# A first k unit of 512 moving tokens in the front, and one hand-ordered section up to the first head

## Chip, core and metric

The kernel runs on one core of a Trainium2 chip. The core's engines are TensorE (PE: matmuls and PE transposes; PEld is its weight load), VectorE (DVE), ScalarE (ACT), GpSimd (POOL) and SyncE (SP, which here issues most DMAs). The metric is the time on the device in microseconds (us), taken over several runs. A profile is one execution of its own with the hardware profiler on; its span runs from the first to the last instruction of the core.

## What is computed

One layer of a hybrid block over 1024 latent tokens with a prefix of 256 context tokens (so 1280 tokens, ten tiles of 128). The input is normalised, modulated by a scale and a shift that come out of a small matrix product with the condition vector, and projected; the projection feeds a gated DeltaNet (branch A) and a differential attention (branch B):

```python
shift, scale, gate = jnp.split(jax.nn.silu(c) @ w_ada + b_ada, 3, axis=-1)
h = rms_norm(x) * (1.0 + scale[:, None]) + shift[:, None]
hc = rms_norm(ctx) * (1.0 + scale_c) + shift_c
qkv_a, z_a, a_raw, b_raw, q_b, k_b, v_b, z_b, gates = split_cols(h @ w_in)
...
qkv = jax.nn.silu(centred_conv(qkv, conv_w)).astype(jnp.float32)
```

Branch A's q, k and v pass a conv over five tokens, SiLU and (q, k) an L2 norm, before its chunked scan over eight heads in two directions. Branch B's v is only stored. All projections are taken in a split form: each operand is the sum of a high and a low part, and three matmuls (high x high, high x low, low x high) stand for one.

## The kernel before, in words

**Front** (`front`). The condition vectors, `w_ada` in four pairs of k tiles (u = 0 to 3, 256 columns each of shift and scale) and the tokens are loaded by SP. Modulation (`modulation`): for u0 and u1 a matmul with two stationary columns and 256 moving ones (`mp<-wa,cT`), for u2 and u3 a form with 32 padded columns that lie in four column groups of PE (`mp<-wa,pad`), folded by a second product. The row sums of squares are ACT's, the reciprocal root is twelve small DVE instructions per group of token tiles (`rms`, L383 to L389). The token tiles are turned by PE transposes, eight k tiles for each of three groups of tokens (0 to 3, 4 to 7, the two of context), group by group (`turns`); ACT and DVE apply the modulation as they evict (`hs`, L409; `hf`, L412), and the low part is a subtraction on DVE for even k and on POOL for odd k (L415). The matmuls of the front (`main`) are **v unit 0**: 256 columns of branch B's v and the 32 columns of the decay and beta inputs, with tokens stationary and 288 weight columns moving, ten token tiles of 24 matmuls. The first group's tiles run through k in parts of four, two and two.

**Conv section** (`conv_start`, `conv_flow`). Twelve units of 256 columns: k, q and v of branch A. Here the weights are stationary and tokens move (512, 512 and, for k and v, 256 columns), 24 matmuls for each of two column tiles and each group of tokens. Five PSUM banks (`pm`) take the results. Each column tile is copied by ACT into one of four rings (L571), goes through a tap on ACT (L581), four on DVE (L583), SiLU (L592), transposes (L597) and, for q and k, a norm, and is stored to DRAM. The ring slot of tile n waits for the stores of tile n - 4. Smaller streams run beside it: the decay (`gates`), lambda, the rotary tables and the row of output gates (`gate_row`: eight loads of 512 KB, each multiplied on DVE).

**Between the sections.** After the conv section the pools on the right are closed; the first head's preparation (`gdn_first`) is written out up to its first need of a PSUM bank (loads of X, kq; 20 Abs and two Exp on ACT), then **v unit 1** follows in plain program order (`unit`, `tok_unit` L501, `v_out` L700 to L703): ten token tiles in five banks, with one staging slot for high and one for low parts. Then the section of scans begins; its PSUM pools take the same banks, and its first product is `gram<-kq`.

**What sets the order.** Inside a `manual_schedule` block the instructions of each engine stand in the order in which a planner calls them: each piece of work is a stream of steps with an engine, a cost in us and the steps that it depends on. `turn_flow` and `flow` pick at each point the stream that can begin first, within a tolerance and by a bias. Before the section of scans the planner's clocks are set to zero. DMA issues are steps of SP's or ACT's own stream, and wait there in order. Only the order is planned: on the chip each instruction waits for semaphores.

Of the kernel before, what the change touches and what calls it, by code (L numbers as in the profile page):

```python
# [17 lines left out]
P = 128  # L18
# [25 lines left out]
class Block:  # L44
# [143 lines left out]
    def setup(self):  # L188
# [7 lines left out]
        self.fold = cp.tile([P, P], F32, name="fold")  # L196
        nc.vector.tensor_reduce(self.fold[:, :32], self.ident.rearrange("p (a i) -> p i a", i=32), AX.X, ALU.add)
        for m in range(1, 4):
            nc.vector.tensor_copy(self.fold[:, 32 * m:32 * m + 32], self.fold[:, :32])
# [37 lines left out]
    def front(self, st, early, kv0):  # L237

        nc, a, cp, V = self.nc, self.a, self.cp, self.nc.vector
        fs, ft = self.spool(st, "fs", 1, side="right"), self.spool(st, "ft", 1, side="right")  # L240
# [3 lines left out]
        for g in range(3):  # L244
            for t in groups[g]:
                xt[t] = fx[g].tile([P, D], F32, tag="x", name="x")
        rows, rw2, rw3 = (fs.tile([n, P], F32, name=i) for i, n in (("rows", 16), ("rw2", 26), ("rw3", 120)))
        smallT = cp.tile([P, 184], F32, name="smallT")
        self.gdn_g, self.diff_g = smallT[:, 40:41], smallT[:, 41:42]
        self.convw = lambda j, t: smallT[:, 64 + j * 24 + t:64 + j * 24 + t + 1]  # L250
        cT = self.cT = cp.tile([P, 16], F32, name="cT")
        c2 = cT.rearrange("p (s k) -> p s k", s=2)
        pad = fs.tile([P, KT, 32], F32, name="pad")
        mods = fs.tile([P, 2, KT, 2], F32, name="mods")
        junk = fs.tile([P, D], mybir.dt.bfloat16, name="junk")
        self.pfree, self.slot_t = [(i, None) for i in range(3)], [None, None]
        turnq, evq, wv = ([], []), [], [self.wv.tile([P, KT, W + 32], F32R, tag=t, name=t) for t in ("wh", "wl")]
        free, self.dq = [None] * self.CB, 2.0
        self.raw_t, self.parts_done, self.parts_, self.part_t = [None, None], 0, {}, {}

# [3 lines left out]
        def loads():  # L264
# [3 lines left out]
            for o in "0s1xw23yk":  # L268
# [5 lines left out]
                elif o in "0123":  # L274
                    u = int(o)
                    for i in range(2):
                        if u == 0:
                            wa[u, i] = self.wab[0].tile([P, KT, W], F32, tag=("wh", "wl")[i], name="wa")
                        elif u == 1:
                            wa[u, i] = self.hc.tile([P, KT, W], F32, tag=f"s2{i}", name="wa")  # L280
                        else:
                            if i == 0:
                                wa[u, 2] = self.hp.tile([P, KT, 512], F32, tag=f"s1{u - 2}", name="wa")
                            wa[u, i] = wa[u, 2][:, :, i * W:(i + 1) * W]
                        T["wa", u, i] = self.later((yield get(3.0, wa[u, i], a["w_ada"][0, :, i * D + u * W:i * D + (u + 1) * W].rearrange(
                            "(k p) n -> p k n", p=P))), -1.2)
                elif o == "w":
                    for s in range(2):
                        k = slice(s * KT // 2, (s + 1) * KT // 2)
                        raws[s] = raw = self.wr.tile([P, KT // 2, W + 32], F32, tag="wr", name="wr")  # L290
                        yield get(1.5, raw[:, :, :W], self.wcols(C_VB).rearrange("(k p) n -> p k n", p=P)[:, k])
                        T["wr", s] = self.later((yield get(0.3, raw[:, :, W:], a["w_in"][0, :, C_AB:C_AB + 32].rearrange(
                            "(k p) n -> p k n", p=P)[:, k])), -1.2)
                elif o == "k":
                    yield lambda: ("w", 1) in T and ("m", 0) in T
                    for s in range(2):
                        k = slice(s * KT // 2, (s + 1) * KT // 2)
                        raws[s] = raw = self.wr.tile([P, KT // 2, W], F32, tag="wr", name="wr")
                        T["kr", s] = yield get(1.5, raw, kv0.rearrange("(k p) n -> p k n", p=P)[:, k], [T["w", s]])
                else:  # L300
                    for t in (range(0, 4), range(4, NT))["xy".index(o)]:
# [3 lines left out]
        def split(dst, key, to, engs):  # L305
            yield lambda: (key, 1) in T
            ends = []
            for s in range(2):
# [7 lines left out]
                if to is T:  # L316
                    T["w", s] = [t1, t2]
# [1670 lines left out]
```

## Time and profile before

| | |
|---|---|
| time, median of 3 runs | 2059.33 us (2055.46 to 2067.66) |
| time of the profiled execution | 2050.87 us |
| its span | 2049.1 us, 38360 instructions |
| granted TensorE clock, mean over the span | 0.985 |
| HBM read and written | 222.66 MB and 112.32 MB |

The page gives the busy time of each engine and a row for each group of instructions: line, engine, operation, output<-input by the program's names, partitions x elements, count, busy time, mean duration in ns, and the idle time of the engine ahead of them with what ended it. Other views answer for a stretch: the busy times by stretch with the granted clock (1.00 is full speed), the instructions in order of time (start, duration), and the chain of work that ended last (start, duration, engine, tile, line). Matmuls overlap in their records, so their pace is read from the distance of their starts.

### The profile page before, as it was taken

To read this page: it belongs to the slowest core of one execution; us is meant where nothing else is said; L and a number is where in the kernel's file an instruction comes from. 1 tells how busy PE (TensorE), PEld (TensorE's weight loads), DVE (VectorE), ACT (ScalarE), POOL (GpSimd) and SP (SyncE) were. 2 spreads that over 40 slices of the span, in tenths; PEclk is the share of its full clock that TensorE was granted. 3 is DMA by queue.
4 is the path that set the end of the run, shared out by engine and by line. 5 is a ranking of instruction groups with operands and counts; after the bars stand their busy time and mean duration, and the time that the engine had idled before them with its cause. 6 is when DMAs were issued, how large, how long until landed. Compare 5 with 4: busy or idle time off the path is not lost.

```text
span 2049.1 us, 38360 instructions
## 1 busy us (share of the span) xinstructions
PE 1968.3 (96%) x14231; PEld 1726.7 (84%) x14231; DVE 1419.5 (69%) x3616; ACT 1053.8 (51%) x2176; POOL 682.3 (33%) x600
## 2 busy tenths in 40 slices
PE   7899999989999998999999999999999999988999
PEld 4788878889999997888787888887888888876899
DVE  4698998847876885657656786227789899874532
ACT  3354344343325443567356754547678888773210
POOL 1100000014431331323323333235566767664122
PEclk9999999999999999999999999999999999999999
DMA  9226543565446556756764764757575666325452
GB/s 316 75 91 159 152 105 87 130 179 158 137 142 207 155 180 170 231 172 213 191 223 131 258 178 146 238 146 220 155 196 134 184 190 160 99 89 194 154 155 85
DMA packets 392030, 337.50 MB, mean 165 GB/s; under 512 B 144431, under 2 KB 343697, under 8 KB 391843
## 3 DMA queue, kind: packets, MB, share of 16 engines
q1 hardware_dynamic: 328963, 275.27, 46.3%
q10 hardware_dynamic: 62880, 59.78, 9.6%
q8 instruction: 112, 1.84, 0.4%
q14 instruction: 75, 0.61, 0.1%
HBM read 222.66 MB, written 112.32 MB: 163 GB/s over the span
## 4 chain that ended last, share of the span: by engine, by line
PE 72%; DVE 10%; DMA 8%; ACT 5%; issue 2%; POOL 1%; SPq 1%; ACTq 0%; DVEq 0%; POOLq 0%
PE mm L55 40%; PE chain L55 5%; PE mo L55 4%; PE s L55 4%; PE v L55 4%; DVE S L1569 3%; PE out L55 3%; PE ma L55 3%; ACT S L1582 2%; PE t L58 2%; DMA ma<-ma 1%; PE mm L501 1%; PE gram L55 1%; DVE al L1643 1%; DMA x<-xd 1%
## 5 line engine op out<-in xcount | busy, mean ns | idle before, releaser
L55 PE MATMUL mm<-hs,wh 128*128 128x512 f32 (+1 forms) x2048 | 644.8, 389 | 0.0
L55 PEld LDWEIGHTS mm<-hs,wh 128*128 128x128 f32 x2048 | 373.2, 190 | 57.6 <-issue 0.9
L55 PE MATMUL mm<-hs,wl 128*128 128x512 f32 (+1 forms) x1024 | 400.0, 391 | 0.0
L55 PE MATMUL mm<-wh,hs 128*128 128x256 f32 (+1 forms) x1632 | 313.2, 290 | 2.6 <-DVE hs L415 2.6
L55 PEld LDWEIGHTS mm<-wh,hs 128*128 128x128 f32 x1632 | 260.8, 194 | 3.8 <-DVE hs L415 3.4
L1569 DVE TENSOR_SCALAR_CACHE_REDUCE S<-s,rsq 128x512 f32<-128x512 f32 (+1 forms) x384 | 241.7, 654 | 32.0 <-PE s L55 29.2
L55 PE MATMUL mm<-wl,hs 128*128 128x256 f32 (+1 forms) x816 | 236.1, 289 | 0.0
L1606 POOL TENSOR_TENSOR S<-S 128x1280 f32<-128x1280 f32 x64 | 188.8, 2952 | 89.3 <-ACT S L1599 81.6
L55 PEld LDWEIGHTS mm<-hs,wl 128*128 128x128 f32 x1024 | 194.6, 190 | 28.2
L1582 ACT ACTIVATE S<-S,mn 128x1280 f32<-128x1280 f32 x128 | 174.7, 1366 | 34.2 <-DVE mn L1581 33.5
L55 PEld LDWEIGHTS mm<-wl,hs 128*128 128x128 f32 x816 | 158.3, 194 | 0.3
L55 PE MATMUL s<-kk,qh 128*128 128x512 f32 (+1 forms) x384 | 145.1, 378 | 3.2 <-DVE S L1569 2.9
L583 DVE SCALAR_TENSOR_TENSOR ac<-xc,smallT,ac 128x1284 f32<-128x1284 f32 (+1 forms) x96 | 138.9, 1449 | 9.5 <-ACT ac L581 8.3
L55 PE MATMUL s<-kk,ql 128*128 128x512 f32 (+1 forms) x384 | 133.8, 359 | 0.0
L1643 DVE TENSOR_TENSOR al<-t,ah 128x512 fp32r<-128x512 f32 (+1 forms) x192 | 107.4, 593 | 9.4 <-ACT ah L1638 8.7
L571 ACT COPY xc<-mm 128x512 f32<-128x512 f32 (+1 forms) x64 | 33.9, 534 | 143.0 <-PE mm L55 133.6
L1164 DVE TENSOR_TENSOR tmp<-ab,ts 80x31 f32<-80x31 f32 (+15 forms) x248 | 100.9, 407 | 8.3 <-DMA ab<-da 2.9
L1638 ACT CAST ah<-t 128x512 fp32r<-128x512 f32 (+1 forms) x192 | 89.8, 515 | 29.0 <-PE t L58 27.8
L568 POOL MEMSET xc<- 128x2 f32 (+1 forms) x64 | 3.5, 100 | 300.6 <-ACT sq L617 152.7
L58 PE MATMUL t<-ct,S 128*128 128x128 f32 x640 | 95.8, 276 | 2.9 <-POOL S L1606 1.6
L1342 DVE SCALAR_TENSOR_TENSOR S<-S,egl,chain 128x128 f32<-128x128 f32 x128 | 43.2, 344 | 75.7 <-PE chain L55 72.7
L1329 ACT ACTIVATE vd<-chain,edk 128x128 f32<-128x128 f32 x144 | 52.2, 368 | 80.7 <-PE chain L55 77.5
(283 smaller groups left out, 4691.6 us busy)
## 6 DMA issues: line engine op xcount, KB each, us to landing
wr<-in_w_in_dram ACTq DMA_DIRECT2D x42, 512.0 KB, 5.5
hx<-in_w_in_dram ACTq DMA_DIRECT2D x64, 256.0 KB, 3.8
X<-gcd SPq DMA_DIRECT2D x16, 640.0 KB, 6.4
kd<-col SPq DMA_DIRECT2D x40, 256.0 KB, 2.5
xd<-X SPq DMA_DIRECT2D x16, 640.0 KB, 6.4
x<-xd SPq DMA_DIRECT2D x80, 128.0 KB, 2.6
kk<-kd SPq DMA_DIRECT2D x32, 320.0 KB, 7.0
wa<-in_w_ada_dram SPq DMA_DIRECT2D x8, 1024.0 KB, 7.2
```

The lines of the kernel that those rows point to most:

```text
L55: self.nc.tensor.matmul(out, lhsT, rhs, start=start, stop=stop)
L58: self.nc.tensor.transpose(out, src, self.ident[:src.shape[0], :src.shape[0]])
L571: e = yield ACT, 0.57 if m == 512 else 0.31, [t, x["old"]], lambda: nc.scalar.copy(xc[:, d:d + m], pt[:, :m])
L583: t = yield DV2, 1.21e-3 * wd, [t], lambda: nc.vector.scalar_tensor_tensor(ac[:, :wd], xc[:, j:j + wd], self.convw(j, x["ct"]), ac[:, :wd] ...
L1164: t = yield DV2, n * w / 960.0 + 0.08, [t, t1], lambda: V.tensor_tensor(tv, ab[:, j + 1:, j:j + 1].to_broadcast([80, n, w]), ts[:, j, :w]. ...
L1329: td = yield ACT, 0.251, [t], lambda: nc.scalar.activation(vd, pc[:, 1], AF.Copy, scale=self.edk[:, c, g:g + 1])
L1342: t = yield DVE, 0.263, [t], lambda: V.scalar_tensor_tensor(Sn, S, self.egl[:, c, g:g + 1], pc[:, 2], ALU.mult, ALU.add)
L1569: e = yield DVE, 0.675 if m == 512 else 0.408, [e, self.sfree[c].get(n - 4 + c)], lambda: self.nc.vector.tensor_scalar(x["S"][c][:, o:o + ...
L1582: x["x"].append((yield ACT, 1.36, [e], lambda: nc.scalar.activation(S, S, AF.Exp, bias=x["mn"][:, c:c + 1], scale=-1.0, accum_out=w["l0"][ ...
L1606: e = yield POOL, 2.9, [e], lambda: self.nc.gpsimd.tensor_tensor(S0, S0, S1, ALU.add)
L1638: e = yield ACT, 0.48 if nb == 4 else 0.27, [t, y["old", k]], lambda: self.nc.scalar.copy(y["ah", k][:, :, q], pv)
L1643: t = yield DVE, 0.603 if k < 2 else 0.322, [e, y["old", k]], lambda: self.nc.vector.tensor_tensor(y["al", k][:, :, q], pv, y["ah", k][:, ...
```

## The change

The first k unit of the conv section and v unit 0 change places. The front's matmuls are now those of the k unit, with weights stationary and a whole group of tokens moving, ordered by pairs of k tiles (`ORDER`): pair 0 for tokens 0 to 3, for tokens 4 to 7, then pair 1, and so on; the context tokens last, over all k. Transposes follow the same order. Five banks hold its results (two column tiles by two groups, and one bank for both context parts). Loads go in a new order: rows, first four x tiles, first k weights, u0, small vectors, four x tiles, u1, u2, u3, context, v's weights. All four modulation pairs take the padded form; the second half's row is evicted by ACT. The reciprocal root is taken per token tile, by POOL (an addition and a power), not on DVE.

v unit 0 becomes the second unit of the conv section (`kind == "t"`), one token tile at a time with 288 columns; its evictions are a stream of the planner, with two staging slots. v unit 1 becomes the last unit of that section, its evictions staged in the conv rings as long as these are open, or in two slots once they are closed. The first head's preparation (`first`) and the load of the rotary table are streams of the same section, which start when all conv tiles and side streams are done. The planner's clocks are not reset ahead of the scans. The gate row is made in two halves of 512 columns (sixteen loads of 256 KB). Constants that only these stages use (`fold`, `convT`, `cT`) lie in a pool of their own that is closed with them.

```diff
-            for o in "0s1xw23yk":
+            for o in "xw0sy123zv":
...
-                        t = yield PE, 0.1 if u >= 2 else 0.432, [T["wa", u, i], tc, tb], lambda: self.mm(
-                            mp[32 * j:32 * j + 32, o:o + W], pad[:, k], wa[u, i][:, k], k < 4, k >= 4) if u >= 2 else self.mm(
-                            mp[:2, o:o + W], c2[:, :, k], wa[u, i][:, k], k == 0, k == KT - 1)
-                    t = yield DVE, 0.42, [t], lambda: V.tensor_copy(mrow[:n, i], mp[:n, o:o + W])
...
+                        t = yield PE, 0.08, [T["wa", u, i], tc, tb], lambda: self.mm(
+                            mp[32 * j:32 * j + 32, o:o + W], pad[:, k], wa[u, i][:, k], k < 4, k >= 4)
...
-            for g in range(3):
...
-                    yield lambda: ("x", t) in T
-                    e = yield ACT, 1.27, [T["x", t]], lambda: nc.scalar.activation(junk, xt[t], AF.Square, accum_out=ss[:, j:j + 1])
...
+            ss, y = (fs.tile([P, NT], F32, name=i) for i in ("ss", "xry"))
+            for t in range(NT):
+                yield lambda: ("x", t) in T
+                e = yield ACT, 1.27, [T["x", t]], lambda: nc.scalar.activation(
+                    junk, xt[t], AF.Square, scale=D ** -0.5, accum_out=ss[:, t:t + 1])
+                e = yield PL1, 0.15, [e], lambda: nc.gpsimd.tensor_scalar_add(y[:, t:t + 1], ss[:, t:t + 1], EPS)
+                e = yield PL1, 0.3, [e], lambda: self.power(y[:, t:t + 1], y[:, t:t + 1])
+                T["xs", t] = yield DVE, 0.69, [e], lambda: V.tensor_scalar_mul(xt[t], xt[t], y[:, t:t + 1])
...
         def turns():
-            for g in range(3):
...
+            for g, ks in ORDER:
+                if g == 2:
+                    yield lambda: ("mm", 1) in T
+                    self.hs.get(2) or self.hgroup(2)
+                for k in ks:
+                    yield lambda: ("m", k // 2) in T and ("xs", groups[g][-1]) in T and self.pfree
...
-            n = 0
-            pts = {}
-            for ts, parts in ((range(4), (range(4), (4, 5), (6, 7))),) + tuple(((t,), (range(KT),)) for t in range(4, NT)):
...
-                            th, tl, o = self.hsel(t)
-                            for i, (ht, wt) in enumerate(((th, wv[0]), (th, wv[1]), (tl, wv[0]))):
-                                e = yield PE, 0.133, [T["h", g, k], T["w", k // 4], b], lambda: self.mm(
-                                    pt[:, :W + 32], ht[:, k, o:o + P], wt[:, k], k == i == 0, k == KT - 1 and i == 2)
...
+            pts = [self.pm.tile([P, 512], F32, tag="mm", name="mm") for _ in range(5)]
+            for g, ks in ORDER:
+                n = len(groups[g]) * P
+                for s, k in [(s, k) for s in range(2) for k in ks]:
+                    yield lambda: ("h", g, k) in T and ("w", k // 4) in T
+                    th, tl, _ = self.hsel(groups[g][0])
+                    pt = pts[4][:, s * W:s * W + W] if g == 2 else pts[2 * s + g]
+                    for i, (wt, ht) in enumerate(((0, th), (0, tl), (1, th))):
+                        e = yield PE, 0.2265 if n == 512 else 0.1195, [T["h", g, k], T["w", k // 4]], lambda: self.mm(
+                            pt, T["hl"][wt][:, k, s * P:(s + 1) * P], ht[:, k, :n], k == i == 0, k == KT - 1 and i == 2)
+                    if k == KT - 1:
+                        self.first_[s, g] = pt, e
+            self.parts_done, self.part_t[0] = 1, e
+
+        ORDER = [(g, (2 * u, 2 * u + 1)) for u in range(4) for g in range(2)] + [(2, range(KT))]
...
+        for g, b in ((self.gates(), 0.5), (self.lam_setup(), 0.6), (self.qk_tables(), 4), (self.gate_row(), 4)):
+            self.stream(self.side(g), b)
+        self.stream(self.conv_weights([c for _, c in cols], pools), 3)
         self.stream(self.conv_flow(cols), 9)
...
-        self.ahead = self.parts_.pop(last)[:2]
-        self.wab = pools if last % 2 == 0 else pools[::-1]
-        self.streams, self.now, self.dq = [], 0.0, 0.0
-        self.clk, self.port, self.table, self.heat = [0.0] * 5, [0.0, 0.0], None, 0.0
+        done = lambda: len(self.cdone) >= self.ctiles and self.sides == 4 and not self.ringed
...
+        self.stream(self.first(done, right, late), 6)
+        self.turn_flow(lambda: last in self.parts_ and self.parts_done == last and self.head and not self.evq)
...
+        self.ahead = self.parts_.pop(last)
+        self.wab = pools if last % 2 else pools[::-1]
+        self.streams = []
+
+    def side(self, g):
+        yield from g
...
+    def first(self, done, right, late):
+
+        self.head = self.late = None
+        yield done
+        for st in right:
+            st.close()
+        self.late = self.tk = late()
+        self.gdn_first()
+        g = self.preps(0)
+        x = next(g)
+        while not callable(x) or x():
+            x = next(g) if callable(x) else g.send((yield x))
+        tb = self.tk.tile([P, 2, 2, NL, 32], F32, tag="tb", name="tb")
+        self.rope["k"] = tb, (yield DMA, 1.5, [], lambda: self.nc.sync.dma_start(tb.rearrange("p a b t f -> p (a b t f)"), self.tbd[1]))
+        self.head = g, x
...
+        free, n, c = [None] * (self.CB - 5), 0, 0
...
+            if kind == "t":
+                w, nt = (W + 32, 1) if i == 1 else (W, 2)
+                for t0 in range(0, NT, nt):
...
+    def v_out(self, pair, t0, nt, pt, t, free):
+
+        nc, V, s, n = self.nc, self.nc.vector, t0 // nt % 2, W * nt
+        ring = None
+        if nt == 2:
+            yield lambda: self.late or self.ctiles + t0 // 2 - 4 in self.cdone
+            ring = None if self.late else self.ctiles + t0 // 2
+        if ring is None:
+            vt, old = [self.tk.tile([P, n], F32R, tag=f"{i}{s}", name="vt") for i in ("ch", "cl")], self.slot_t[s]
+        else:
+            self.ringed, old = self.ringed + 1, self.out_t[ring - 4]
+            vt = self.cv.tile([P, CW + 2 * PAD], F32, tag="xc", name="vx")[:, :2 * n].bitcast(F32R).rearrange("p (i c) -> p i c", i=2)
...
+        acc = cv.tile([P, 512], F32, name="gacc", bufs=1)
+        t = t1 = None
         for o in (0, 512):
...
-                self.tk = self.spool(cx, "tk2")
...
-                first, head = self.gdn_first(gr, zr)
...
-                self.unit(*v1, self.wcols(self.part_cols(*parts[0])))
...
+                cols = kv[:1] + [("t", C_VB)] + kv[1:] + [("t", C_VB + W), (None, self.part_cols(*parts[0]))]
...
+                    self.gstack = gr, zr
+                    self.conv_start(cols, (right, lc), lambda: self.spool(cx, "tk2"))
+                    first, head = self.head
```

410 lines of the change are left out of this document (175 added, 235 removed).

## The prediction

> **What bounds the kernel now.** I read the page's busy table first, then the busy times of stretches cut where the work changes, then the chain that ended last around the two places where TensorE (PE) stands idle.
>
> ```profile
> span 2049.1 us, 38360 instructions
> PE 1968.3 (96%) x14231; PEld 1726.7 (84%) x14231; DVE 1419.5 (69%) x3616; ACT 1053.8 (51%) x2176; POOL 682.3 (33%) x600
> PE 72%; DVE 10%; DMA 8%; ACT 5%; issue 2%; POOL 1%; SPq 1%; ACTq 0%; DVEq 0%; POOLq 0%
> ```
>
> PE is busy for 96% of the span and carries 72% of the last chain, so time is won only where PE idles, or runs at a low clock: 81 us are idle in all. The busy times by stretch show where (columns: stretch, length, busy time and count of PE, PEld, DVE, ACT, POOL, then granted clock, DMA share, GB/s):
>
> ```profile
> 0.00:92.89 92.89, 74.31 (x476) 55.43 (x476) 53.83 (x131) 35.50 (x59) 17.95 (x19) 0.93 0.60 200
> 92.89:410.87 317.98, 316.22 (x1590) 267.22 (x1589) 276.91 (x399) 135.43 (x161) 3.55 (x64) 1.00 0.48 121
> 410.87:439.70 28.83, 28.83 (x243) 28.83 (x242) 11.80 (x11) 10.75 (x25) 3.04 (x2) 1.00 0.74 189
> 446.91:454.90 7.99, 0.01 (x2) 0.04 (x1) 5.47 (x11) 5.94 (x14) 3.66 (x2) 0.72 0.33 110
> 454.90:460.00 5.10, 5.10 (x24) 5.10 (x25) 0.83 (x2) 0.58 (x1) 0.00 (x0) 0.50 0.48 156
> 460.00:464.00 4.00, 4.00 (x33) 4.00 (x33) 1.74 (x6) 0.92 (x3) 0.00 (x0) 0.92 0.39 131
> ```
>
> The front (v unit 0) ends at 92.89 and idles PE for 18.6 us. The twelve k, q and v units run to 410.87 with PE full, and v unit 1 to 439.70. Then comes a hole of 7.99 us, after which 5.10 us run at half clock (2.55 us lost) and 4 us at 0.92 (0.3 lost): the hole costs 10.9 us.
>
> **The change part by part.** *Unit costs.* The timeline gives PE's pace in steady work:
>
> ```profile
> 80.75 0.42 PE L55 MATMUL mm<-wh,hs 128*128 128x288 f32 x2
> 92.75 0.29 PE L55 MATMUL mm<-wh,hs 128*128 128x288 f32 x1
> 399.16 0.62 PE L55 MATMUL mm<-hs,wh 128*128 128x512 f32 x2
> 407.32 0.62 PE L55 MATMUL mm<-hs,wh 128*128 128x512 f32 x2
> 408.00 0.40 PE L55 MATMUL mm<-hs,wh 128*128 128x256 f32 x2
> 410.87 0.28 PE L501 MATMUL mm<-wh,hs 128*128 128x256 f32 x1
> ```
>
> Between the first two rows stand 90 matmuls of 288 columns in 12.00 us, so 0.133 us each; between the next two 36 of 512 columns in 8.16 us, 0.227 each; then 24 of 256 columns in 2.87 us, 0.120 each. So v unit 0 is 240 x 0.133 = 32.0 us of PE, and the first k unit 96 x 0.227 + 48 x 0.120 = 27.5 us.
>
> *The swap.* The first k unit goes into the front and v unit 0 behind it. If F is the time at which the front's last matmul ends, PE, kept full, comes to the end of v unit 1 at F + 32.0 + (317.98 - 27.5) + 28.83 = F + 351.3. Before, that was 439.70. So the swap gains 88.4 - F.
>
> *When the loads let the front end.* The DMA engines are saturated there (DMA view of the first 100 us, 40 slices of 2.5 us):
>
> ```profile
> DMA  2799999999999999999100311104003012233396
> GB/s 60 209 366 344 340 349 389 410 366 295 334 349 349 348 363 408 411 395 347 43 0 0 105 52 52 56 5 152 0 0 97 15 52 90 67 105 108 39 322 201
> ```
>
> ```profile
> wa<-in_w_ada_dram SPq DMA_DIRECT2D x8, 1024.0 KB, 7.2
> x<-in_x_dram SPq DMA_DIRECT2D x8, 512.0 KB, 10.0
> wr<-in_w_in_dram SPq DMA_DIRECT2D x4, 512.0 KB
> ```
>
> The first 17 slices sum to 14.2 MB at 42.5 us. The new order puts 13.9 MB up to the last modulation weights: constants and rows 0.3, eight x tiles 4.2, two halves of the first k weights 1.05, eight modulation loads 8.4. They land at about 42 us by the same curve. Behind them come the two context tiles and v's weights (47 to 48 us), needed later.
>
> *What PE still owes then.* In the changed kernel's order on PE, behind the last modulation product (8 matmuls, seen as 16) stand 67 of the 96 matmuls of 512 columns, 37 transposes and the 48 of 256 columns. The pieces (timeline, then the chain):
>
> ```profile
> 32.78 1.07 PE L55 MATMUL mp<-wa,pad 128*32 128x256 f32 x16 [0.79 <-DVE mods L359]
> 46.02 0.44 PE pt L58 x4
> ```
>
> That is 1.1 + 0.3 (folding) + 67 x 0.227 + 37 x 0.11 + 48 x 0.120 = 26.4 us. PE comes to that product when the weights have landed (42) and when VectorE (DVE) and GpSimd (POOL) have delivered the third k pair before it; I take 44. So F is 70.4 at full clock. By the same prices PE has only some 15 us of work between 21 and 44, so I add 2 us for a low clock: F = 72.4.
>
> *DVE beside it.* These groups of the first 93 us, by form, must fit in front of it:
>
> ```profile
> L412 DVE TENSOR_SCALAR hf<-pt,mods 128x512 f32<-128x512 f32 x16 | 12.9, 809 | 4.5 <-ACT hs L409 3.6 <-POOL hs L415 0.5
> L391 DVE TENSOR_SCALAR x<-x,xry 128x1024 f32<-128x1024 f32 x10 | 7.0, 746 | 0.0
> L415 DVE TENSOR_TENSOR hs<-hf,hs 128x512 fp32r<-128x512 f32 x8 | 5.5, 684 | 0.0
> L412 DVE TENSOR_SCALAR hf<-pt,mods 128x256 f32<-128x256 f32 x8 | 4.3, 544 | 1.0 <-ACT hs L409 0.7
> L313 DVE TENSOR_TENSOR wl<-wr,wh 128x1024 fp32r<-128x1024 f32 x2 | 2.4, 1222 | 0.0
> L353 DVE COPY mrow<-mp 128x256 f32<-128x256 f32 x4 | 1.7, 420 | 2.7 <-PE mp L55 2.7
> L415 DVE TENSOR_TENSOR hs<-hf,hs 128x256 fp32r<-128x256 f32 x4 | 1.7, 415 | 0.0
> ```
>
> From about 21.5 us (modulation of the first k pair ready) DVE owes 12.9 + 6 x 0.746 + 5.5 + 4.3 + 2.4 + 1.7 + 1.7 = 33 us, with the small modulation adds 34. Walked in its new order with its waits for landings, it is done near 62 us; 26 matmuls of 256 columns then remain (3 us). So DVE alone would allow F = 66, and PE sets F. **Bounds of F:** 66 (DVE) to 82: of PE's 26 us, 31 wide matmuls and 21 transposes (9.4 us) stand ahead of the point where the last k pair is awaited, and at half clock they would take 9.4 us more. The swap gains 88.4 - 72.4 = **16 us** (6 to 22).
>
> *The joined section.* The hole before is read from the timeline:
>
> ```profile
> 428.36 1.96 SPq L1096 DMA_DIRECT2D X<-gcd  x2
> 434.33 5.96 ACT L1113 ACTIVATE X<-X,gcc 128x128 f32<-128x128 f32 x20 [10.66 <-DMA X<-gcd]
> 444.89 0.56 ACT L700 CAST vt<-mm 128x512 fp32r<-128x512 f32 x1
> 454.10 0.69 DVE L701 TENSOR_TENSOR vt<-mm,vt 128x512 fp32r<-128x512 f32 x1 [2.29 <-DMA vd<-vt]
> 454.90 2.05 PE L55 MATMUL gram<-kq 128*128 128x128 f32 x8 [7.99 <-issue]
> ```
>
> The gram product takes the bank of v unit 1's fourth tile, and its eviction stands on ScalarE (ACT) behind the head's 20 Abs and two Exp, with one staging slot that waits for each store. In the changed order three of the five evictions stand ahead of the Abs, the fourth behind one Abs alone, and there are more slots; the gram waits for the fourth eviction and for kq. Counting from v unit 1's start, the last conv tile's stores leave at about 15 us (two evictions of 0.69 us now stand among the last taps on DVE), X is issued at 20.6, lands 6 us later as before (428.36 to 434.33), so that the fourth eviction is done at 28.4 and kq, issued 2 us behind X, lands near 31. PE arrives at 28.8. A stall of 2 to 3 us remains, against 10.9: **8 us** gained (0 to 10.9).
>
> *Edits at about nothing.* The modulation of the first two k pairs changes from 3.6 us per 16 instructions to 1.07, and the reciprocal roots move from DVE to POOL; both lie under the loads. The root on 128x1 isn't in the trace: between 0.10 us (a memset of 128x1) and 1.76 (the same operation on 128x8); I take 0.3, and even the upper end delays only the x tiles, which DVE awaits with 8 us of waits in hand. The gate row becomes 16 loads and 16 multiplies at half width, the same sum, under a DVE that has 41 us free in 318. v unit 0's evictions add 10 x (0.42 + 0.18) = 6 us of DVE to that section; where that cover is gone, PE waits for banks. From the second head on, each engine's order is that of before, so the shift should arrive at the end whole.
>
> ```profile
> 447.79 1.76 POOL L172 TENSOR_TENSOR ss<-ss,mhalf 128x8 f32<-128x8 f32 x1 [1.48 <-DVE ss L984]
> 0.72 0.10 POOL L201 MEMSET mhalf<- 128x1 f32 x1 [0.29 <-POOLq L1975]
> 19.45 3.62 PE L55 MATMUL mp<-wa,cT 128*2 128x256 f32 x16
> ```
>
> **Sum:** 16 + 8 = 24 us. The profiled execution took 2050.87 us (span 2049.1 and 1.8 around it), so 2027 on its own level. It lies 0.4% under the median of the runs shown, 2059.33 (2055.46 to 2067.66). On the median's level the forecast is **2035 us**.
>
> **The rivals.**
>
> *A, the hole stays.* kq lands late, or the head's ACT work again holds the fourth eviction. For it: X can't be issued before the last conv stores. Against: the order above. Gain 16 alone: 2043 us.
>
> *B, the front runs at half clock.* This row pair shows what it costs: three matmuls of 288 columns from 69.48 to 70.37, 0.89 us against 0.40.
>
> ```profile
> 69.48 0.85 PE L55 MATMUL mm<-wh,hs 128*128 128x288 f32 x2 [2.31 <-DVE hs L415]
> 70.37 0.68 PE L55 MATMUL mm<-wh,hs 128*128 128x288 f32 x2
> ```
>
> The new front has PE wait for pairs of loads 6 us apart until 42 us, so it may come to its 26 us of work cold and be stopped again by DVE in between. With F = 82 the gain is 6.4 + 8 = 14: 2045 us. The Trainium skill (TensorE: Matmul & The Clock Gate, section "What's actually happening") says that an idle window of about 3.4 us halves the clock and a window of sustained work restores it. By that rule, the trace agrees: the hole of 7.99 us is followed by 0.50, and full clock is back within 9 us. The same rule speaks for B where PE's gaps exceed that window, and against it from 44 us on, where PE has a queue of 26 us in front of it.
>
> *A and B together:* 6 us, 2053 us.
>
> *C, DVE chained to the v units; slower.* Fifteen evictions now stand in DVE's order among the conv taps, and each can hold DVE until its tile's matmuls end. Work of DVE from F to the end of v unit 1: 276.9 + 11.8 + 6.0 = 294.7 us, waits before 41, together 335.8 of 351.3: 15.5 us of slack. If DVE did nothing else between evictions, v unit 0 would add 32 - 6 = 26 us of waits and v unit 1 some 25: 51 us, 35.5 beyond the slack, and 11.5 more than the gain: 2071 us. It decides from 15.5 + 24 = 39.5 us of added waits. Against it: the new order on DVE puts conv taps and norms between the evictions.
>
> *The change doesn't do what it says:* 67 of the 96 wide matmuls still stand behind the last load, so "begins with" is only a third true; the forecast holds that already.
>
> **How the numbers follow.** Forecast 0.50 (own range 2026 to 2042), A 0.16, B 0.16, both 0.10, C 0.08. A measurement of this kernel can tell about 0.5%, 10 us, from no change: below 2049 is faster, above 2069.6 slower. The forecast, A and B are faster: 0.82, less 0.02 for their edges, 0.80; both together and half of C's cases within 0.5%: 0.13 with the edges; slower 0.07. The range reaches from a front at its lower bound (22) with two thirds of the hole gone, 30 us or more and some for the level, 2020, to A and B together, 2053.
>
> **What would show it.** The first 288-column matmul of v unit 0 starts at F: 72 (66 to 82), where before the first k unit started at 92.89. PE stays full from there to the gram (between F + 351 and F + 354; 454.9 before, 424 to 427 now), and the clock behind it stays near 1.00. If the time from the gram to the end differs from before's by more than 3 us, the claim that the shift arrives whole is wrong; if PE has gaps between F and the gram, C is at work.

## The result, and the profile after

| | before | changed |
|---|---|---|
| time, median | 2057.39 us (2048.15 to 2067.66, 4 runs) | 2033.60 us (2031.96 to 2036.39, 4 runs) |
| timed again later | 2056.70 us (17 runs) | 2037.30 us (2032.64 to 2040.16, 6 runs) |
| profiled execution, span | 2050.87 us, 2049.1 us | 2031.96 us, 2030.2 us |

The changed kernel is faster: the ratio is 0.9885 (95% interval 0.9835 to 0.9934), and 0.9899 (0.9878 to 0.9920) the second time, so 21 to 24 us. The forecast was 2035 us, 24 us below the 2059.33 that were known then. The ratios leave out two slow runs, 2733.54 us of the kernel before and 7830.38 us of experiment 6.

The page of the changed kernel, with its span, its busy times and the shares of the chain that ended last:

```profile
span 2030.2 us, 38407 instructions
PE 1959.4 (97%) x14239; PEld 1722.5 (85%) x14239; DVE 1407.7 (69%) x3581; ACT 1058.0 (52%) x2184; POOL 688.7 (34%) x618
PE 72%; DMA 10%; DVE 8%; ACT 5%; issue 2%; SPq 1%; POOL 1%; ACTq 0%; DVEq 0%; POOLq 0%
```

PE now idles 71 us of its span instead of 81, and its busy time is 9 us less.

Where the work changes (stretch, length, busy time and count of PE, PEld, DVE, ACT, POOL, granted clock, DMA share, GB/s), and the first rows of v unit 0, of v unit 1 and of the gram in the timeline:

```profile
0.00:74.85 74.85, 57.63 (x387) 41.61 (x388) 41.07 (x69) 36.84 (x59) 28.76 (x48) 1.00 0.67 232
74.85:395.73 320.88, 320.64 (x1687) 275.55 (x1686) 279.04 (x420) 137.43 (x169) 3.23 (x54) 1.00 0.46 118
395.73:424.50 28.77, 28.77 (x242) 28.75 (x240) 14.94 (x20) 10.93 (x20) 0.63 (x1) 1.00 0.95 236
424.50:440.00 15.50, 14.69 (x124) 14.48 (x123) 7.60 (x21) 11.51 (x30) 2.75 (x2) 1.00 0.89 300
```

```profile
74.85 0.30 PE L55 MATMUL mm<-wh,hs 128*128 128x288 f32 x1
...
395.73 0.28 PE L55 MATMUL mm<-wh,hs 128*128 128x256 f32 x1
...
420.54 0.57 ACT L546 CAST vt<-mm 128x512 fp32r<-128x512 f32 x1
...
424.55 0.46 PE L55 MATMUL gram<-kq 128*128 128x128 f32 x2
...
425.81 0.94 PE L55 MATMUL gram<-kq 128*128 128x128 f32 x6 [0.81 <-DMA kq<-gq]
```

The front's matmuls end at F = 74.85 us, v unit 1 starts F + 320.9 and ends at 424.5, where it ended at 439.70 before: the swap is worth 15.2 us there. v unit 1's fourth eviction (the CAST at 420.54) stands behind one Abs of the head, as the prediction read it from the order, and the gram follows at once, without the 7.99 us of idle and the half clock behind it; PE then waits 0.8 us for kq. Before, 7.2 us of the next unit's work stood ahead of the gram (439.70 to 446.91), so the gram's own time (30.4 us sooner) says too much. A fair mark behind the rearranged stretch is the first product of 64 columns of the first head's inverse (the first `pz<-X` on 64 rows): 619.3 us before, 595.6 now, **23.7 us**. The span is shorter by 18.9 us only, since later stages took longer; that is taken up behind experiment 8.

### The profile page after: what moved, and what is told of

The parts are those of the page before. It is cut to its first block, busy times and chain, and to the rows that moved or that the text cites. A ratio compares the mean times of both kernels' runs of the same rounds, so it can differ in the third digit from the quotient of the medians.

```text
span 2030.2 us, 38407 instructions
## 1 busy us (share of the span) xinstructions
PE 1959.4 (97%) x14239; PEld 1722.5 (85%) x14239; DVE 1407.7 (69%) x3581; ACT 1058.0 (52%) x2184; POOL 688.7 (34%) x618
## 4 chain that ended last, share of the span: by engine, by line
PE 72%; DMA 10%; DVE 8%; ACT 5%; issue 2%; SPq 1%; POOL 1%; ACTq 0%; DVEq 0%; POOLq 0%
PE mm L55 37%; PE chain L55 5%; PE mo L55 4%; PE s L55 4%; PE v L55 4%; PE m L55 4%; PE out L55 3%; PE ma L55 3%; DVE S L1557 3%; PE t L58 2%; ACT S L1570 2%; DMA wr<-in_w_in_dram 1%; DVE al L1631 1%; DMA vv<-gv 1%; PE gram L55 1%
## 5 line engine op out<-in xcount | busy, mean ns | idle before, releaser
L55 PE MATMUL mm<-wh,hs 128*128 128x256 f32 (+1 forms) x1792 | 334.8, 286 | 0.0
L55 PEld LDWEIGHTS mm<-wh,hs 128*128 128x128 f32 x1792 | 281.5, 191 | 0.4
L55 PE MATMUL mm<-wl,hs 128*128 128x256 f32 (+1 forms) x896 | 256.0, 286 | 0.0
L55 PEld LDWEIGHTS mm<-wl,hs 128*128 128x128 f32 x896 | 171.2, 191 | 0.3
L590 DVE SCALAR_TENSOR_TENSOR ac<-xc,convT,ac 128x1284 f32<-128x1284 f32 (+1 forms) x96 | 138.7, 1448 | 16.2 <-ACT ac L588 15.6
```

Source lines behind the costliest of these rows:

```text
L55: self.nc.tensor.matmul(out, lhsT, rhs, start=start, stop=stop)
L590: t = yield DV2, 1.21e-3 * wd, [t], lambda: nc.vector.scalar_tensor_tensor(ac[:, :wd], xc[:, j:j + wd], self.convw(j, x["ct"]), ac[:, :wd] ...
```

## The experiments

Twelve runs, of which 8 and 9 are the second profiles. F is read as in the prediction (the first 288-column matmul), P is the first 64-column product just named. The ratios are against the kernel before, on the same chip.

| kernel | F | gram | P | ratio of times (95%) |
|---|---|---|---|---|
| before, first and second profile | – | 454.9, 455.9 | 619.3, 619.8 | 1 |
| changed, first and second profile | 74.85, 74.23 | 424.5, 424.8 | 595.6, 595.1 | 0.9885, 0.9899 |
| 1 swap alone | 74.20 | 439.6 | 604.6 | 0.9949 (0.9933 to 0.9965) |
| 2 join alone | – | 446.9 | 617.9 | 1.0004 (0.9985 to 1.0023) |
| 3 groups, not pairs | 80.71 | 430.8 | 601.4 | 0.9916 (0.9897 to 0.9936) |
| 4 idle transposes ahead | 75.59 | 426.8 | 598.1 | 0.9909 (0.9889 to 0.9929) |
| 5 less loads | 75.56 | 426.8 | 597.2 | one run, 2041.09 us |
| 6 old modulation form | 85.63 | 434.8 | 605.4 | 0.9961 (0.9943 to 0.9979) |
| 7 idle transposes in the gaps too | 74.25 | 427.5 | 599.5 | 0.9902 (0.9873 to 0.9931) |
| 10 first modulation unit first | 76.51 | 428.0 | 600.2 | 0.9896 (0.9870 to 0.9922) |
| 11 and the second one early | 75.16 | 425.9 | 597.1 | 0.9887 (0.9862 to 0.9913) |
| 12 join alone, DVE relieved | – | 454.5 | 620.4 | one run, 2093.98 us |

**1. The swap alone.** The new front, with v unit 1 and the first head in plain program order as before:

```diff
-cols = kv[:1] + [("t", C_VB)] + kv[1:] + [("t", C_VB + W), (None, self.part_cols(*parts[0]))]
+cols = kv[:1] + [("t", C_VB)] + kv[1:] + [(None, C_VB + W)]
...
+first, head = self.gdn_first(gr, zr)
...
+self.unit(*v1, self.wcols(self.part_cols(*parts[0])))
```

> The new front with v unit 0 moved behind the first k unit, but v unit 1 and the first head's preparation outside the hand-ordered section, as before the change. Forecast's theory (two independent gains, 15 us measured for the swap and 9 us for the hole): v unit 1 still starts near 396 us, the hole before the gram comes back with 8 us of idle PE and half clock behind it, and the time is 14 to 16 us under the kernel before. Rival (the two parts need each other: the swap only fills the time in which the head's loads were waited for): under 8 us, with v unit 1 itself late. Rival (the join was worth nothing by itself): the same time as the changed kernel, 22 to 24 us under the kernel before.

Its first 64-column product comes at 604.6, 14.7 us sooner than before, and the hole is back (PE's waits between 74 and 446 us, then the stretch behind the gram's start, then the mark P):

```profile
PE gram L55 <- issue: 9.1, 1, 9.1
```

```profile
439.60:446.00 6.40, 6.35 (x31) 6.38 (x32) 1.77 (x5) 0.58 (x1) 0.00 (x0) 0.53 0.40 135
```

```profile
L55 PE MATMUL pz<-X x320: 218/218/268, 604.6 to 1273.3; 64*64 64x64 f32 x160
```

So at P the two parts of the changed kernel are 14.7 and 9.0 us, near the 16 and 8 of the forecast. In the time the swap alone shows 10.5 us (7 to 14), which misses the 14 to 16 expected; the 4 us that are lacking lie in stages behind P (1440.4 us from P to the end, against 1429.8 and 1434.8 in the two profiles of the kernel before).

**2. The join alone.** The old front, with v unit 1 and the first head in the hand-ordered section; from P on the orders of DVE, ACT and POOL are those of the changed kernel.

```diff
-self.conv_start(kv, C_VB + W)
...
+cols = kv + [("t", C_VB + W), (None, self.part_cols(*parts[0]))]
...
+self.conv_start(cols, (right, sv), lambda: self.spool(cx, "tk2"))
```

> The old front (v unit 0 first, its modulation forms and roots as before), with v unit 1 and the first head's preparation joined to the hand-ordered section. Forecast's theory: the front's PE still ends at 92.9 us, v unit 1 still ends near 440 us, and the gram follows it at once: 8 to 10 us under the kernel before, so that this and the swap alone add up to 22 to 26 us. Rival (the hole only moves, to the landing of kq or to a DVE order with more waits): 0 to 4 us.

The rival came out: nothing is gained (ratio 1.0004, P 1.4 us sooner), since DVE has an order with more waits. The profiled execution took 2065.44 us, 10 more than the median of its 12 runs; the excess lies behind P (1445.7 us from there to the end). The hole ahead of the gram is gone, but the conv section has got one of its own. PE's main waits from 90 to 450 us (`pq` is a product of the norms), the stretch that holds the first two, and rows of DVE ahead of it and in it:

```profile
PE mm L55 <- DVE wl L935: 2.7, 1, 2.7
PE pq L55 <- DVE zk L705: 2.4, 1, 2.4
PE gram L55 <- DMA kq<-gq: 0.7, 1, 0.7
```

```profile
280.00:300.00 20.00, 15.21 (x53) 12.06 (x54) 19.62 (x37) 5.28 (x7) 0.13 (x2) 0.83 0.71 157
```

```profile
257.43 0.69 DVE L692 TENSOR_SCALAR rq<-pq 32x8 f32<-32x8 f32 x4 [4.54 <-PE pq L55]
...
287.09 1.55 DVE L650 SCALAR_TENSOR_TENSOR ac<-xc,smallT,ac 128x1284 f32<-128x1284 f32 x1
...
288.79 1.22 DVE L935 TENSOR_TENSOR wl<-wr,wh 128x1024 fp32r<-128x1024 f32 x1
```

DVE is busy 19.62 of those 20 us, and the low part of the next weights (`wl`) stands behind conv taps in its queue; PE waits, and its clock falls to 0.83. P of the four kernels makes the sum: 14.7 (swap) + 1.4 (join) = 16.1, and both together 23.7. The missing 7.6 us fit this stall, 4.8 us of idle PE in these 20 us and a low clock in the rest; no run shows the join on the old front with neither the stall nor the hole. The changed kernel has 0.24 us of idle PE from F to the end of v unit 1. The forecast priced the join only on top of the swap; as a part by itself it is worth nothing here.

**12. The join alone, DVE relieved.** To see whether it is DVE's load that stalls PE there:

```diff
-                                       c0, W, [self.part_t.get(i - 2)], self.parts_, i, (DV2, DV2))
+                                       c0, W, [self.part_t.get(i - 2)], self.parts_, i, (POOL, DV2))
```

> The join alone (old front, v unit 1 and first head joined), with the low part of every unit's first half of weights subtracted on POOL, which is idle in the conv section, instead of DVE: some 13 x 1.2 us less for DVE between 93 and 440 us. The planner writes another order for the scans from this, so only the time of the first gram product is read. Theory (the old front leaves DVE behind, and PE then waits for the low parts of its weights: 5.2 us of idle PE and a low clock near 290 us): the idle goes and the gram starts at 440 to 443 us instead of 446.9. Rival (the joined order itself, not DVE's load, holds PE): 446 to 449 us.

PE's busy time of the stretch from 200 to 300 us, and from 440 to 460:

```profile
200.00:300.00 100.00, 100.00 (x496) 83.94 (x495) 89.85 (x126) 42.30 (x49) 10.60 (x20) 1.00 0.45 115
...
440.00:460.00 20.00, 14.67 (x104) 13.90 (x103) 4.00 (x13) 10.78 (x27) 0.63 (x1) 0.83 0.80 278
```

The stall in the conv section is gone (PE 100.00 of 100 us). DVE is as busy as before from 280 to 300 us (19.72 of 20 us), which speaks for the place of `wl` in its queue, behind the taps, rather than for its load as such; the edit changes the planner's order too, so this isn't fully shown. But the gram started at 454.5, not at 440 to 443, and P is 620.4, 1 us later than in the kernel before. The head's X is issued only at 444.62 us there, behind v unit 1's last store from a ring and two stores of the rotary table, and PE idles 5.3 us between 440 and 460. Half of the theory held; that the gain would then arrive didn't. The run took 2093.98 us with another order in all later stages, which says nothing on the join.

**3. Groups instead of pairs.**

```diff
-ORDER = [(g, (2 * u, 2 * u + 1)) for u in range(4) for g in range(2)] + [(2, range(KT))]
+ORDER = [(g, (2 * u, 2 * u + 1)) for g in range(2) for u in range(4)] + [(2, range(KT))]
```

> The changed kernel with the first k unit's contraction in the order of token groups (all eight k tiles of the first four token tiles, then all eight of the next four) instead of by pairs of k tiles over both groups. Theory (the pairs feed PE while the modulation weights land): work ahead of the last modulation product is only the first group's, some 28 us from 15.2 us on, so PE waits 2 to 3 us for the last weights and the front's matmuls end near 77 us instead of 74.85; 2 to 3 us slower than the changed kernel. Rival (PE has enough to do in either order): 74 to 75.5 us, no difference.

F is 80.71: the pairs are worth 6 us of F, more than the 2 to 3 expected, and not for the expected reason. In the time they are worth 3.5 us by the ratios, with intervals that overlap. From 30 us on PE waits 3 us in all, none of it for the last weights but for evictions (the longest is 1.8 us for DVE's `hf`), and it falls below full clock (0.89 between 45 and 60 us):

```profile
45.00:60.00 15.00, 12.99 (x78) 9.41 (x77) 9.25 (x14) 9.39 (x15) 7.24 (x8) 0.89 0.02 4
```

**5, 6. What sets F.** The prediction had the last modulation weights land at 42 us, and PE's remaining work behind them. Theory A is that. Theory B is that PE's own work sets F. Experiment 5 leaves out the last 2 MB of modulation weights; experiment 6 puts the first two units' products and their folding back into the old form.

```diff
+if u == 3:
+    wa[u, i] = wa[2, i]
...
```

> The changed kernel without the two loads of the fourth modulation unit's weights (2 x 1 MB): its products read the third unit's weights, so this part of the output is another. The instructions of PE, DVE, ACT and POOL stand in the same order, and the last weights land some 5 us sooner. Theory A (the last weights' landing sets the front's end): the first 288-column matmul starts at 70 to 71 us instead of 74.85. Theory B (PE's own work from 15.2 us on, a part of it at half pace, sets it): 74 to 75 us, unchanged, although the weights are there sooner.

```diff
-mp[32 * j:32 * j + 32, o:o + W], pad[:, k], wa[u, i][:, k], k < 4, k >= 4)
+mp[32 * j:32 * j + 32, o:o + W], pad[:, k], wa[u, i][:, k], k < 4, k >= 4) if u >= 2 else self.mm(
+mp[:2, o:o + W], c2[:, :, k], wa[u, i][:, k], k == 0, k == KT - 1)
```

> The changed kernel with the modulation of the first two k pairs in its form of before the change (two output rows, 3.62 us per unit half in the trace of before, against 1.94 us now), every engine's order kept. Theory A, with the prediction's step that this edit lies under the loads and is worth nothing: the front's matmuls end within 1 us of 74.85. Theory B (PE's work sets the end): four unit halves cost 1.7 us more each, the front's matmuls end at 80 to 82 us and the time is 5 to 7 us over the changed kernel's.

With less loads F stays, though DMA's traffic ends 5 us sooner (40 to 45 us: share 0.07, where the changed kernel has 1.08). The first row of v unit 0 there:

```profile
75.56 0.30 PE L55 MATMUL mm<-wh,hs 128*128 128x288 f32 x1
```

With the old form F is 85.63, 11 us later, and the kernel 12 to 13 us slower than the changed one (0.9961 against 0.9899), twice what theory B expected:

```profile
16.30 6.46 PE L55 MATMUL mp<-wa,cT 128*2 128x256 f32 x16 [10.37 <-DMA wa<-in_w_ada_dram]
23.48 3.62 PE L55 MATMUL mp<-wa,cT 128*2 128x256 f32 x16
...
34.19 4.37 PE L55 MATMUL mp<-wa,cT 128*2 128x256 f32 x16
...
85.63 0.30 PE L55 MATMUL mm<-wh,hs 128*128 128x288 f32 x1
```

The four old products take 6.46, 3.62, 4.37 and 3.62 us, where the changed kernel's take 1.94 three times and 1.07: 11.2 us more. (Each is 8 matmuls, which the trace records as 16.) Theory A falls: the landing of the last weights doesn't set F, and an edit that the prediction put at nothing is worth some 11 of the swap's 15 us. In the changed kernel PE has no idle from 30 to 60 us:

```profile
15.00:30.00 15.00, 12.74 (x71) 7.09 (x72) 7.10 (x12) 6.20 (x11) 5.98 (x9) 1.00 1.07 395
30.00:45.00 15.00, 15.00 (x133) 10.40 (x133) 8.67 (x15) 5.69 (x9) 4.66 (x4) 1.00 1.08 372
45.00:60.00 15.00, 15.00 (x95) 11.85 (x94) 11.80 (x16) 10.15 (x17) 9.10 (x8) 1.00 0.02 5
60.00:74.85 14.85, 14.61 (x93) 12.11 (x92) 7.72 (x16) 6.51 (x11) 4.15 (x15) 1.00 0.28 78
```

The fourth of these products shows where PE's work takes over. First row: the changed kernel; second: experiment 5; third: experiment 7 (below).

```profile
32.83 1.07 PE L55 MATMUL mp<-wa,pad 128*32 128x256 f32 x16
...
33.53 1.07 PE L55 MATMUL mp<-wa,pad 128*32 128x256 f32 x16
...
32.21 1.07 PE L55 MATMUL mp<-wa,pad 128*32 128x256 f32 x16
```

From its start to F it is 42.02 us in the changed kernel, 42.03 in experiment 5, 42.04 in 7, 42.00 in 4 and 41.63 in 10; in 6 it starts at 41.09 and takes 2.55 us more itself, and the distance is 44.54. So from there on PE's own work sets F, whether the loads end at 40 or at 45 us, and what moves F is the time at which PE comes to this product. (In experiment 5 it came 0.7 us later, since its first weights were there 1.3 us later.)

**4, 7, 10, 11. Can F be moved?** If PE's work from its first weights at 15.2 us sets F, then full pace from the start, or an earlier start, should bring it forward. Experiment 4 puts 60 transposes of the identity ahead of the first weights, experiment 7 puts 75 there and 47 more in the gaps until 28 us, experiments 10 and 11 load modulation weights sooner.

```diff
+for _ in range(60):
+    self.tr(wm[:, 0:P], self.ident)
```

> The changed kernel with 60 transposes of the identity on PE, whose results nobody reads, put behind its first transpose, so that PE is busy from about 6 us until the first modulation weights land at 15.2 us. Everything else stands in the same order. Theory A (the last weights' landing at 42 to 45 us sets the front's end, as the prediction worked it out): PE reaches the last modulation product at best 2 us sooner, and the front's matmuls end at 73 to 75 us. Theory B (PE's own work sets it: it idles 2.2 of the 59.7 us from 15.2 us on, and runs at half pace until 31 us): up to half of the 13.6 us of PE time before 31 us is saved, the matmuls end at 68 to 70 us, and the time is 5 to 7 us under the changed kernel's. Rival C (the idle PE isn't what makes the pace low at 15 us): 16 products still take 1.9 us and nothing changes.

```diff
+WARMTH = {9: 4, 11: 5, 23: 2, 31: 9, 32: 13, 35: 10, 43: 4}
...
+self.keep(self.WARMTH.get(self.npe, 0))
...
+self.keep(75)
```

> As the kernel with 60 idle transposes ahead of the first modulation weights, which came to full pace at 15.4 us and fell back to half at 19.5 us in the gaps; now 75 of them stand there and 47 more in the gaps that PE has between 16 and 28 us, so that it shouldn't fall back. Theory B (PE's work and its pace set the front's end): PE is at full pace from 15 us on and the front's matmuls end 2 to 5 us sooner than 74.85, at 70 to 73 us. Theory A (the landing of the last weights, near 45 us, and the 28 us of PE work behind it): not below 73 us. Rival C (the gaps are too wide, or idle transposes don't hold the pace): half pace from about 20 us on, 75 us or later.

```diff
-for o in "xw0sy123zv":
+for o in "0xwsy123zv":
```

> The changed kernel with the two loads of the first modulation unit ahead of the first four x tiles and the first k weights, instead of behind them; the bytes up to the last modulation weights are the same. Theory B (PE's work from the arrival of its first weights sets the front's end): PE starts near 10 us instead of 15.2, has the first unit's products out of the way before the x tiles are there, and the front's matmuls end 1.5 to 4 us sooner, at 71 to 73.5 us. Theory A (the landing of the last modulation weights sets it): unchanged at 74 to 75 us. Rival (x is late): the first hs comes 5 us later and the end at 77 to 79 us.

```diff
-for o in "xw0sy123zv":
+for o in "0xws1y23zv":
```

> As the kernel before this one, and the second modulation unit's two loads also ahead of x tiles four to seven. Theory B: if PE's work is the limit and not the second group's x tiles, the end comes no later than with the first unit alone, 70 to 74 us. Rival (the second group's x tiles, 5 us later, keep PE waiting): 76 to 79 us. Theory A: 74 to 75 us.

None of the four does it: F is 75.59, 74.25, 76.51 and 75.16, and no ratio lies outside the changed kernel's interval. In experiment 4 the first product runs at full pace (1.07 us), but the pace has fallen back by 20.6 us (8 transposes in 1.95 us), though no single gap of PE there was over 1.4 us, and it stays low until 33 us:

```profile
15.38 1.07 PE L55 MATMUL mp<-wa,pad 128*32 128x256 f32 x16 [1.31 <-DMA wa<-in_w_ada_dram]
...
20.58 1.95 PE L58 MATMUL pt<-ct,x 128*128 128x128 f32 x8
...
27.12 1.94 PE L55 MATMUL mp<-wa,pad 128*32 128x256 f32 x16 [0.57 <-DMA wa<-in_w_ada_dram]
```

```profile
20.00:25.00 5.00, 3.42 (x14) 2.51 (x13) 3.45 (x8) 4.66 (x9) 2.49 (x5) 0.50 1.05 390
```

The Trainium skill (TensorE: Matmul & The Clock Gate, section "A second HAM failure mode: psum-queue depth-cycling") describes a kernel that idles for short times between groups of matmuls often enough to be throttled again. By that rule, the trace agrees: PE is busy 3.42 of 5 us and the granted clock is 0.50. In experiment 7 PE is at full pace from 16.81 us on (every product 1.07 us), and its start, behind 75 transposes, was 1.6 us later. The pace gained little: the second matmul of 512 columns waits for DVE's `hs` (the modulated tokens) in both kernels and starts at the same time (first row: the changed kernel), and behind it stand 14 idle transposes, 1.5 us at 0.11 us each.

```profile
26.18 0.79 PE L55 MATMUL mm<-hs,wh 128*128 128x512 f32 x1 [1.45 <-DVE hs L403]
...
26.20 0.50 PE L55 MATMUL mm<-hs,wh 128*128 128x512 f32 x1 [0.25 <-DVE hs L416]
```

From its first product to F it takes 57.4 us, where the changed kernel takes 59.65. In experiment 10 PE starts at 7.26 us, but the x tiles come later, and the first matmul of 512 columns runs at 25.21 us instead of 23.94.

So theory B in the form "start plus a fixed time" falls too. What these kernels have in common: from about 33 us on (38 in experiment 11, whose order is another) PE is full, and F follows from the work that is left to it there. How much is done by then hangs on several things that lie close together: the arrival of the x tiles and of `hs` behind them, that of the first weights, the pace. In these four experiments F moved by less than 2 us; work added to PE moves it fully (experiment 6), and no run takes work away. Which of them would be the next limit isn't settled.

**8, 9. Both kernels again.** The stages from the scans on have nearly the same instructions in the same order; only a few dozen rows of the merge stage stand in another order.

> The changed kernel itself, timed again beside the kernel before, to narrow the ratio, and with a second profile, to see how far the stages whose instructions stand in the same order differ from one execution to the next. If the 6 us by which the first profile's stages from the scans to the end were longer than in the one of before are chance, this profile's stages lie on both sides of it; if they belong to the changed kernel, they are as long again: 1434 to 1436 us from the first head's 64-column inverse products to the end, against 1429.8 before.

> The kernel before itself, with a second profile. All profiles taken with the changed kernel and its variants have 89.3 to 90.1 us from the first to the last of the final projection's matmuls and 437.8 to 440.6 us for the attention stage, where the first profile of the kernel before had 87.2 and 436.3 with the same instructions. If that was this one execution, its second profile has 89 to 90 and 438 to 441, and its span is 2053 to 2057 us; if it belongs to the kernel, 87.2 and 436 again.

From P to the end it was 1429.8 and, again, 1434.8 us before, 1434.6 and 1435.8 in the changed kernel. So most of the loss between the first two profiles can be chance of one execution, as far as two profiles of each tell: the attention stage took 436.3 and then 440.4 us in the kernel before (1399.4 to 1835.7, and the first row below), 438.5 both times in the changed one. The projection at the end doesn't look like chance. First row: attention of the kernel before, second profile; then its final projection; then that of the changed kernel's second profile.

```profile
1400.50:1840.90 440.40, 425.67 (x2740) 370.43 (x2739) 369.10 (x1248) 345.25 (x577) 289.37 (x143) 0.98 0.57 156
...
1963.10:2050.30 87.20, 87.08 (x767) 86.84 (x767) 22.70 (x44) 6.86 (x12) 23.99 (x12) 1.00 0.41 126
```

```profile
1937.50:2026.80 89.30, 89.30 (x767) 89.27 (x766) 22.01 (x43) 6.66 (x12) 23.92 (x12) 1.00 0.38 122
```

The final projection takes 87.2 us in both profiles of before and 89.3 in both of the changed kernel, with the same matmuls in the same order. The expectation on the second profile of before held for the attention stage and the span (2054.6 us) and was wrong for the projection.

## Why the prediction was right, and where not

- **The sum**, 16 + 8 = 24 us to 2035 us: measured 23.8 us between the first medians (20.8 by the second ratio), and 14.7 + 9.0 = 23.7 at P. Both terms have about the forecast size.
- **F = 72.4 (66 to 82)**: 74.85. PE came to the last modulation product at 46.99 us, 3 us later than the 44 forecast, and from there to F it took 27.9 us at full pace, 1.5 more than the 26.4 of the sum. The 2 us added for a low clock were not spent there; they covered most of these errors, which is luck. The formula from F to the end of v unit 1, F + 351.3, gave 426.2; it was 424.5, mostly because PE had 0.24 us of idle there, not the 1.76 us that the section had before.
- **"They land at about 42 us ... I take 44"**: this step failed as a cause. All loads of the front had ended by 45 us (47 to 48 forecast); by the GB/s of the changed kernel's trace the 13.9 MB up to the last modulation weights were moved by about 39 us, an estimate. So PE came to the last product some 8 us behind them, by its own work, and experiment 5 takes 2 MB away and F stays. The number came out near because the work behind the last product was counted nearly rightly, and 44 happened to lie near the time at which PE was through with its own work.
- **"Edits at about nothing", the modulation form**: this step failed most. It was reasoned from the old front, where PE idles 18.6 us; in the new one PE is full, and experiment 6 puts the edit at 11 us of F. Without it the swap would be worth 4, by this difference. The forecast's F took in only the last product and had the others lie under the loads, so that the sum wasn't hurt by the price of nothing. The root on POOL measured 0.66 us on 128x1 (0.3 taken, 0.10 to 1.76 given); putting it back on DVE wasn't tried.
- **DVE done near 62 us**: its last step of the front ended at 69.1. With the 3 us of matmuls that the prediction puts behind it, DVE would have allowed F = 72.2, so PE still set F, with 2.6 us in hand instead of the 6 forecast.
- **The hole, 8 us (0 to 10.9)**: it closed better than forecast, with 0.8 us of waiting instead of 2 to 3, and 9.0 us at P. Rival A is out. That it needs the swap was not foreseen (experiment 2).
- **Rival B**, the front at half clock, happened until 31 us and not behind it. **Rival C**, DVE chained to the v units: PE is idle 0.24 us from F to the gram. It is the join with the old front that shows DVE holding PE, for 5 us, and there the waits name the norms (2.4 us) and the next weights' low part (2.7 us), not the v units' evictions.
- **"The shift should arrive at the end whole"**: by the sign that was named it failed. From the gram to the end it took 1594.2 us before and 1605.7 in the changed kernel, 11.5 us more, where 3 were allowed. But 7.2 us of it is the next unit's work, which stood ahead of the gram before and stands behind it now, so the gram was a bad mark. From P on it is 4.8 us more in the first pair of profiles and 1.0 in the second, while two executions of the kernel before differ by 5.0. Of the 23.7 us at P in the first pair 18.9 arrive at the end, of the 24.7 in the second 23.7 (2054.6 to 2030.9). Of a loss behind P, only the 2.1 us of the projection show in both.

## What to carry to other kernels

An edit that is thought to hide behind a wait must be priced again when the change takes the wait away: the padded modulation form was put at nothing from a front in which PE waited, and was worth 11 us where PE was full. Two parts that are each sound need not add up: the join gained 9 us at P on the new front and 1.4 on the old one, where DVE was late with the next weights. To learn what ends a stretch, take the suspected thing away (here the last loads) before the number built on it is trusted, even when that number came out right.

## What the runs showed beside it

- The granted clock column shows 1.00 from the start of the changed kernel, though its matmuls ran at half pace until 31 us (a modulation product in 1.94 us at 15.2 and 27.75 us, in 1.07 at 32.83). So at the start of these traces the durations tell the pace and the column doesn't; in experiment 4, after 20 us, the column has 0.50 for the same 1.94 us.
- The final projection's 256-column matmuls follow each other at 87.2 / 767 = 0.114 us in both profiles of the kernel before and at 0.116 in both of the changed one, at a granted clock of 1.00 and without idle time in either. From the first to the last of the 768 it is 87.4 us before and 89.5 changed, and 89.5 to 90.6 in the variants (92.8 in experiment 12, with 1.9 us of waits). The cause is open; no experiment here was aimed at it.
- A modulation product in the two-column form took 6.46 us at half pace and 3.62 at full pace; in the padded form 1.94 and 1.07.
- Transposes alone brought PE to full pace: in experiment 4 the first 19 of the 60 follow each other at 0.21 us and the others at 0.11. With 47 more of them in the gaps of experiment 7 the pace held, and every modulation product took 1.07 us.
